# Hybrid attention and mLSTM block on one core: weights' sums, the norm of the far blocks and a gate moved in the program order

## The chip, the cores and the metric

The kernel runs on one core of a Trainium2 chip. The metric is the device time of one execution in microseconds (us), the median of the runs; lower is better. A core has a matrix engine (TensorE, PE in the profile, with its weight loads shown apart as PEld), a vector engine (VectorE, DVE), a scalar engine (ScalarE, ACT), GpSimd (POOL) and SyncE (SP), from which this kernel issues all its DMAs. Each engine works through its instructions in program order and waits on semaphores for the others.

## The reference, cut to what matters

```python
xn = rms_norm(x, mix_norm_g)                    # x: (1, 2048, 1024), one layer
aq, ak, av, mq, mk, mv, mo, i, f, ga, gm = split(xn @ w_in)
att = chunk_band_attention(aq, ak, av, rel_bias)          # 8 heads of 64, chunks of 64
hm = mlstm_chunkwise(silu(conv(mq)), silu(conv(mk)), mv, i + b_i, f + b_f)
hm = rms_norm(hm, mh_norm_g)                              # per head, 4 heads of 128
mlstm_out = sigmoid(mo) * hm
y = sigmoid(ga) * (att @ w_att_proj) + sigmoid(gm) * (mlstm_out @ w_mlstm_proj)
x = x + y @ w_out
x = x + square(relu(rms_norm(x) @ w_up)) @ w_down
out = rms_norm(x, final_norm_g)
```

Everything is float32. A matrix product is made of three products of float32r parts (high by high, high by low, low by high), so each operand is first split into two parts.

## The kernel before, in words

**Blocks and spans.** The 2048 tokens are four blocks of 512; two blocks are a span. Blocks 0 and 1 are projected plainly, one after the other (`dense`, L625): value tiles, gates, query, key and conv tiles, then `ga` tiles, then the two projections of the mixers. From there on both blocks of a span go together through products by a 2x2 scheme with seven products instead of eight (`quad`, L542): each quad is 7 products of 24 matmuls of 128x512, 168 in all. In order of time these stages are here called G0 and G1 (gate `gm` of the first span), O0 and O1 (`w_out` of the first span), then the second span's input projections gm0, gm1, q, mq, vm0, ga0, k, vm1, mk, ga1, mo (`IN_ORDER`, L51), then up0.0 to up0.7, the down products of the first span (`down`, L598) with the attention and the recurrence of blocks 2 and 3 beside them, and O1, up and down of the second span.

**Operands.** A quad needs seven combinations of the four quarters of its activations. `take_parts` (L1697) makes them: for each k of four it takes five tiles of the pool `ctx`, loads four quarters (L1706), scales them where a norm's gain is due (L1709), makes four sums on DVE (L1719) and splits each of seven into a tile pair (ACT L953, DVE L958). k above 1 waits until k - 2 is split. `norm_far` (L863) makes the normed input of blocks 2 and 3 for it: it loads 32 tiles of 256 KB, squares 16 of them on ACT, scales 16 on DVE (L899) and stores these 16.

**Weights.** They need the same seven combinations. There are two ways. The sum: `sum_w` (L374) loads the four quarters of half a quad (256 KB each, L384), makes four differences on DVE (L389) and stores them in DRAM (`wsum`); the loader then loads each of the seven parts (512 KB, L402). The second difference of a half waits until the first is stored. The quad form: `quad_w` (L426) loads the four quarters (512 KB, L397) into the four buffers `wraw` and makes the differences there on DVE (L439, 128x1024); for the up products of the first span it stores them too (`keep`, L434), since the second span loads them again. Either way each part is split by ACT (L420) and DVE (L422).

**Taking results off.** The banks of a quad are reused: `combine` (L1732) copies or adds a product into `ctx` (ACT L1742, DVE L1750), and the next product of that bank waits for it. `after_out` adds at L1987, `add_down` at L2187. For `mo`, `finish` of `after_in` (L1900) applies tanh on ACT (L1914) and then (t + 1) times a gain on GpSimd (L1919), and stores the tile to `mfar` (L2026).

**The order.** All of this is written as threads, and a planner (`Flow`, L92) decides in which order their instructions are written down: it keeps an estimated clock for each engine and takes the ready step that could start first; equal starts go by the thread's priority. Each step names its engine, an estimated duration and, for a load, an estimated time until it lands: `yield "sp", 900, 2000` is 0.9 us of issue and 2.0 us more to landing. A further layer then places the instructions on the engines. The estimates change no wait: they set the order alone. Side work (sums, `norm_far`) is spawned with a low priority at a point of `dense`: in the kernel before, `norm_far` after the mixer inputs of block 0 (L656), the sums of G and O weights at the end of block 0, those of the two `vm` quads at the end of block 1 (L666), and those of the eight down quads at the places `D_SUMS` (L53) of the second span's projections (L691) and of up0 (L711).

Of the kernel before, what the change touches and what calls it, by code (L numbers as in the profile page):

```python
# [51 lines left out]
N_REC = 1  # L52
D_SUMS = (3, 6, 9, 11, 12, 13, 14, 15)  # L53
PROJ = {2: (4,0), 3: (6,2)}
# [37 lines left out]
class Flow:  # L92
# [77 lines left out]
    def run(self):  # L170
        while self.ready or self.blocked:
            moved = True
            while moved:
                moved = False
                for th in sorted(self.blocked, key=lambda x: (x.prio, x.n)):
                    ok, value = self._grant(th)
                    if ok:
                        self.blocked.remove(th)
                        self.now = th.at
                        self._step(th, value)  # L180
                        moved = True
            if not self.ready and not self.blocked:
                break
            if not self.ready:
                raise RuntimeError("no thread can go on")
            best = None
            for th in self.ready:
                t, frm = th.at
                for e in th.req[0].split("|"):
                    start = t + self.LAT[frm].get(e, 0.0)  # L190
                    if e == "pe" and th.prio < 5:
                        start += self.SLACK
                    key = (max(self.clock[e], start), th.prio, th.n)
                    if best is None or key < best[0]:
                        best = (key, th, e)
            (start, _, _), th, e = best
            self.ready.remove(th)
            end = start + th.req[1]
            self.clock[e] = end
            if len(th.req) > 2:  # L200
                end += th.req[2]
            th.at = self.now = (end, e)
            self._step(th, e)


def act_ns(n, ps=False, ap=0):
    return (51 if ps else 93) + 0.834 * n + 93 * ap
# [11 lines left out]
class Layer:  # L219
# [98 lines left out]
    def weights(self):  # L318
# [13 lines left out]
        for s in range(NS):  # L332
            if s == 1:
                yield from (part(q, m) for q in range(N_G, N_G + N_O) for m in range(7))
            for q in range(N_G + N_O, N_G + N_O + N_F):
                if s == 0:
                    yield "quad", (q, True)
                else:
                    yield from (part(q, m) for m in range(7))
# [34 lines left out]
    def sum_w(self, q):  # L374

        fl, V = self.fl, self.nc.vector
        for h in range(2):
# [4 lines left out]
            for n, x in ((0, a), (1, c), (3, d), (2, b)):  # L382
                yield "sp", 900, 2000
                self.nc.sync.dma_start(x, wf[n])  # L384
# [240 lines left out]
    def dense(self):  # L625
        fl = self.fl
        none = [None] * KT
        for b in range(2):
# [25 lines left out]
            if b == 0:  # L654
                fl.spawn(self.norm_in(1), 3)
                fl.spawn(self.norm_far(), 3)  # L656
            for j in range(8):
# [4 lines left out]
            if b == 1:  # L662
                G = self.operands()
                for k in range(4):
                    fl.spawn(self.take_xn(0, k, *G), 2)
            early = range(N_G + N_O) if b == 0 else range(Q_VM, Q_VM + 2)  # L666
            for q in early:
                fl.spawn(self.sum_w(q), 3)
# [21 lines left out]
        for i, name in enumerate(IN_ORDER):  # L690
            if i in D_SUMS:  # L691
                fl.spawn(self.sum_w(N_Q - N_F + D_SUMS.index(i)), 3)
            last = name == IN_ORDER[-1]
# [9 lines left out]
        for s in range(NS):  # L703
# [6 lines left out]
            for i in range(N_F):  # L710
                if s == 0 and len(IN_ORDER) + i in D_SUMS:  # L711
                    fl.spawn(self.sum_w(N_Q - N_F + D_SUMS.index(len(IN_ORDER) + i)), 3)
                if i == 2:
# [983 lines left out]
    def take_parts(self, src, kept, scale, k, A, aev, g=None):  # L1697
        fl, V = self.fl, self.nc.vector
        if k > 1:
            yield "wait", [aev[m][k - 2] for m in range(7)]  # L1700
        got = yield "get", self.ctx, 5
        a11, a12, a21, a22, s1 = (x[:, :512] for x in got)
        for b, j, a in ((0, k, a11), (0, 4 + k, a12), (1, k, a21), (1, 4 + k, a22)):
            yield "wait", [kept[b][j]]
            yield "sp", 900, 2000
            self.nc.sync.dma_start(a, src[b].ap()[j])  # L1706
# [15 lines left out]
        yield "wait", done  # L1722
        fl.put(self.ctx, *got)

# [6 lines left out]
    def combine(self, finish, o=0):  # L1731
# [6 lines left out]
        def copied(n, name, ps, clear):  # L1738
            (t,) = yield "get", self.ctx, 1
            held[n][name] = t  # L1740
            yield "act", act_ns(512, True)
            nc.scalar.copy(t[:, o:o + 512], ps)  # L1742
# [3 lines left out]
        def summed(n, name, to, ps, clear):  # L1746
            yield "wait", [ev[n][name]]
            t = held[n][name]
            yield "dve", dve_ns(512)
            nc.vector.tensor_add(t[:, o:o + 512], ps, t[:, o:o + 512])  # L1750
# [148 lines left out]
    def after_in(self, name):  # L1899
        fl, nc = self.fl, self.nc  # L1900

        def finish(n, which, t, ps):
# [14 lines left out]
            if name == "mo":  # L1917
                yield "pool", 670
                nc.gpsimd.tensor_scalar(t5, t5, 1.0, self.ghead[:, j:j + 1], op0=ALU.add, op1=ALU.mult)  # L1919
                dst, ev = self.mfar[b].ap()[2 * MH + j], self.m_ev[b, 2 * MH + j]  # L1920
# [35 lines left out]
    def after_out(self, s, q, U):  # L1956
# [24 lines left out]
        def add(n, w, done, ps, clear):  # L1981
# [3 lines left out]
            t = xt[n][w][:, :512]  # L1985
            yield "dve", dve_ns(512)
            V.tensor_add(t, ps, t)  # L1987
# [177 lines left out]
    def add_down(self, s, m, j, ps):  # L2165
# [9 lines left out]
        else:  # L2175
# [7 lines left out]
            for to, frm in steps:  # L2183
                if to not in acc:
                    (acc[to],) = yield "get", self.ctx, 1
                yield "dve", dve_ns(512)
                V.tensor_add(acc[to][:, :512], ps, acc[frm][:, :512])  # L2187
# [128 lines left out]
    def build(self):  # L2316
# [19 lines left out]
        self.wev, self.wgot = collections.defaultdict(Event), collections.defaultdict(Event)  # L2336
        self.td_ev = {q: E(2) for q in (*range(N_G + N_O), *range(N_Q - N_F, N_Q + 2))}
        self.t_ev = [[E(4) for _ in range(7)] for _ in range(NS)]
# [112 lines left out]
```

## Time and profile before

| | |
|---|---|
| median of 3 runs | 2897.58 us (2896.61 to 2900.97) |
| the profiled execution | 2903.79 us |
| its span, first to last instruction | 2901.7 us |
| mean granted clock of TensorE | 0.993 |
| DMAs | 629.87 MB, queue q1 busy 65.4% of 16 engines' span |
| instructions of `sum_w`'s differences (L389) | 112, of quad form's (L439) 60 |

The page gives busy times by engine, groups of instructions by line, and for each the idle time of the engine before them with what ended it. The windows view gives the busy time, number of instructions and granted clock in any stretch; the waits view who waited for whom; the timeline single instructions with, in brackets, the idle time of their engine just before and what ended it.

### The profile page before, as it was taken

To read this page: it belongs to the slowest core of one execution; us is meant where nothing else is said; L and a number is where in the kernel's file an instruction comes from. 1 tells how busy PE (TensorE), PEld (TensorE's weight loads), DVE (VectorE), ACT (ScalarE), POOL (GpSimd) and SP (SyncE) were. 2 spreads that over 40 slices of the span, in tenths; PEclk is the share of its full clock that TensorE was granted. 3 is DMA by queue.
4 is the path that set the end of the run, shared out by engine and by line. 5 is a ranking of instruction groups with operands and counts; after the bars stand their busy time and mean duration, and the time that the engine had idled before them with its cause. 6 is when DMAs were issued, how large, how long until landed. Compare 5 with 4: busy or idle time off the path is not lost.

```text
span 2901.7 us, 39144 instructions
## 1 busy us (share of the span) xinstructions
PE 2827.3 (97%) x13576; PEld 2351.1 (81%) x13576; DVE 2035.9 (70%) x3778; ACT 1549.2 (53%) x2690; POOL 67.6 (2%) x124
## 2 busy tenths in 40 slices
PE   8999999999999999999999999999899999999998
PEld 7888878887787888877888888788778888888887
DVE  6886579867884865876666787769877744455565
ACT  4665356644453544565555575446645755554444
POOL 0000000000000000020000000000000000000000
PEclk9999999999999999999999999999999999999999
DMA  6328963368974566668877966688468855576563
GB/s 214 99 94 296 318 204 95 103 229 301 306 240 139 200 217 218 203 218 293 291 273 257 272 205 189 200 243 273 147 212 293 270 193 186 188 255 201 192 220 136
DMA packets 287238, 629.87 MB, mean 217 GB/s; under 512 B 31936, under 2 KB 46400, under 8 KB 287040
## 3 DMA queue, kind: packets, MB, share of 16 engines
q1 hardware_dynamic: 287040, 627.38, 65.4%
q8 instruction: 106, 1.74, 0.2%
q14 instruction: 92, 0.75, 0.1%
HBM read 437.46 MB, written 189.79 MB: 216 GB/s over the span
## 4 chain that ended last, share of the span: by engine, by line
PE 75%; DVE 10%; DMA 7%; ACT 4%; issue 3%; POOL 1%; SPq 0%; POOLq 0%; DVEq 0%; ACTq 0%
PE bank L564 33%; PE bank L481 11%; PE bank L482 11%; PE bank L483 11%; PE bank L592 2%; DVE wsp L422 2%; PE bank L1210 2%; PE bank L1245 1%; PE bank L1276 1%; DVE r L958 1%; DMA r<-u 1%; ACT wsp L420 1%; DMA wsum<-ctx 1%; DVE sc L1251 1%; DMA tmp<-in_x 1%
## 5 line engine op out<-in xcount | busy, mean ns | idle before, releaser
L564 PE MATMUL bank<-r,wsp 128*128 128x512 f32 x5208 | 1197.6, 391 | 22.0 <-DVE ctx L1750 9.6
L564 PEld LDWEIGHTS bank<-r,wsp 128*128 128x128 f32 x5208 | 979.7, 189 | 234.2 <-DVE ctx L1750 11.9
L422 DVE TENSOR_TENSOR wsp<-wraw,wsp 128x1024 fp32r<-128x1024 f32 x461 | 563.2, 1222 | 359.5 <-ACT wsp L420 349.2
L420 ACT CAST wsp<-wraw 128x1024 fp32r<-128x1024 f32 x461 | 484.0, 1050 | 526.7 <-PE bank L482 220.7
L481 PE MATMUL bank<-r,wsp 128*128 128x512 f32 x1600 | 640.0, 400 | 1.5 <-DVE scs L1251 0.8
L482 PE MATMUL bank<-r,wsp 128*128 128x512 f32 x1600 | 625.6, 391 | 0.0
L483 PE MATMUL bank<-r,wsp 128*128 128x512 f32 x1600 | 625.5, 391 | 0.0
L483 PEld LDWEIGHTS bank<-r,wsp 128*128 128x128 f32 x1600 | 300.7, 188 | 64.9
L481 PEld LDWEIGHTS bank<-r,wsp 128*128 128x128 f32 x1600 | 301.5, 188 | 54.3 <-DVE tmp L1222 1.2
L482 PEld LDWEIGHTS bank<-r,wsp 128*128 128x128 f32 x1600 | 301.8, 189 | 52.4 <-DVE r L958 0.2
L1750 DVE TENSOR_TENSOR ctx<-bank,ctx 128x512 f32<-128x512 f32 x174 | 118.6, 686 | 91.9 <-PE bank L564 90.3
L953 ACT CAST r<-r 128x512 fp32r<-128x512 f32 x224 | 136.6, 622 | 76.0 <-DMA r<-u 63.1
L958 DVE TENSOR_TENSOR r<-r 128x512 fp32r<-128x512 f32 x224 | 149.3, 687 | 36.5 <-ACT r L953 35.5
L1742 ACT COPY ctx<-bank 128x512 f32<-128x512 f32 x174 | 101.1, 582 | 68.1 <-PE bank L564 63.9
L1260 ACT ACTIVATE sc<-sc,scs 128x640 f32<-128x640 f32 (+4 forms) x128 | 97.4, 761 | 69.8 <-DVE scs L1257 68.5
L389 DVE TENSOR_TENSOR ctx<-ctx,ctx 128x512 f32<-128x512 f32 x112 | 76.4, 689 | 66.5 <-DMA ctx<-in_wf 37.9
L1210 PE MATMUL bank<-r,r 128*128 128x256 f32 (+1 forms) x672 | 111.1, 284 | 6.8 <-DVE r L1281 6.2
L2121 ACT ACTIVATE ctx<-ctx 128x512 f32<-128x512 f32 x96 | 60.6, 631 | 102.6 <-DVE ctx L1750 102.5
L1210 PEld LDWEIGHTS bank<-r,r 128*128 128x128 f32 x672 | 98.7, 191 | 20.2 <-DVE r L1281 9.9
L1251 DVE CUSTOM_DVE_ANT_0 sc<-bank,bias 128x320 f32<-128x320 f32 (+3 forms) x240 | 105.6, 459 | 7.8 <-PE bank L1245 6.8
L1281 DVE TENSOR_TENSOR r<-bank,r 128x512 fp32r<-128x512 f32 (+1 forms) x168 | 96.3, 593 | 10.4 <-ACT r L1279 9.7
L953 ACT CAST r<-ctx 128x512 fp32r<-128x512 f32 x116 | 69.5, 618 | 61.2 <-DMA ctx<-xn 30.2
(274 smaller groups left out, 2906.1 us busy)
## 6 DMA issues: line engine op xcount, KB each, us to landing
wraw<-in_wf SPq DMA_DIRECT2D x168, 512.0 KB, 4.2
wraw<-wsum SPq DMA_DIRECT2D x144, 512.0 KB, 4.1
r<-u SPq DMA_DIRECT2D x224, 256.0 KB, 4.2
wraw<-in_w SPq DMA_DIRECT2D x104, 512.0 KB, 3.8
u<-ctx SPq DMA_DIRECT2D x128, 256.0 KB, 2.7
ctx<-in_wf SPq DMA_DIRECT2D x112, 256.0 KB, 4.5
wsum<-ctx SPq DMA_DIRECT2D x112, 256.0 KB, 3.7
u<-tmp SPq DMA_DIRECT2D x96, 256.0 KB, 3.2
```

What stands on the lines that cost most here:

```text
L420: nc.scalar.copy(w[:, 0], raw)
L422: nc.vector.tensor_sub(w[:, 1], raw, w[:, 0].bitcast(F32))
L481: mm(ps, lh, rh, start=first, stop=False)
L482: mm(ps, lh, rl, start=False, stop=False)
L483: mm(ps, ll, rh, start=False, stop=last)
L564: mm(ps, wv[:, x, k, n], a[:, y], start=new and k == 0 and x == y == 0, stop=k == 3 and x == 1, skip_group_check=True)
L953: self.nc.scalar.copy(dst[:, 0], src)
L958: self.nc.vector.tensor_sub(dst[:, 1], src, dst[:, 0].bitcast(F32))
L1210: nc.tensor.matmul(bk[:, c0:c0 + w], st, sl[:, x, o:o + w], start=n == 0, stop=n == total - 1)
L1251: nc.vector.tensor_tensor_reduce(out=e[:, x * w:x * w + w], in0=bks[x][:, :w], in1=br[:, j0 + x * w:j0 + x * w + w], op0=ALU.add, op1=ALU. ...
L1742: nc.scalar.copy(t[:, o:o + 512], ps)
L1750: nc.vector.tensor_add(t[:, o:o + 512], ps, t[:, o:o + 512])
```

## The change

1. `norm_far` is spawned after the mixer inputs of block 1 and not of block 0.
2. The sums of the two `vm` quads are spawned at places 1 and 2 of the second span's projections, and not at the end of block 1.
3. The first two up quads of the first span (`N_USUM`) change from the quad form to sums, spawned at places 4 and 5; their parts are loaded seven by seven. The eight down sums move to places 7, 9 and 11 to 16.
4. The estimate of the landing of loads in `take_parts` and `sum_w` goes from 2000 to 3500 ns.
5. `take_parts` takes the five tiles of odd k from the pool `temp` (6 tiles) where the scale is 1.
6. Steps that free a bank (`combine`, `after_out`, `add_down`) go ahead of others that could start at the same time (`"dve!"`, `"act!"`: priority -1).
7. The gain of `mo` is applied on ACT (Identity with scale and bias g, that is g t + g) and not on GpSimd.

```diff
+N_USUM = 2
+EARLY_SUMS = {1: Q_VM, 2: Q_VM + 1, 4: N_G + N_O, 5: N_G + N_O + 1}
+EARLY_SUMS.update({i: N_Q - N_F + n for n, i in enumerate((7, 9, 11, 12, 13, 14, 15, 16))})
...
+                    prio = th.prio
+                    if e[-1] == "!":
+                        e, prio = e[:-1], -1
...
-                    key = (max(self.clock[e], start), th.prio, th.n)
+                    key = (max(self.clock[e], start), prio, th.n)
...
-                if s == 0:
+                if s == 0 and q >= N_G + N_O + N_USUM:
                     yield "quad", (q, True)
...
-                yield "sp", 900, 2000
+                yield "sp", 900, 3500
                 self.nc.sync.dma_start(x, wf[n])
...
             if b == 0:
                 fl.spawn(self.norm_in(1), 3)
+            else:
                 fl.spawn(self.norm_far(), 3)
...
-            early = range(N_G + N_O) if b == 0 else range(Q_VM, Q_VM + 2)
-            for q in early:
+            for q in range(N_G + N_O if b == 0 else 0):
                 fl.spawn(self.sum_w(q), 3)
...
-            if i in D_SUMS:
-                fl.spawn(self.sum_w(N_Q - N_F + D_SUMS.index(i)), 3)
+            if i in EARLY_SUMS:
+                fl.spawn(self.sum_w(EARLY_SUMS[i]), 3)
...
-        got = yield "get", self.ctx, 5
+        pool = (self.ctx, self.temp)[k % 2 if scale == 1.0 else 0]
+        got = yield "get", pool, 5
...
-            yield "sp", 900, 2000
+            yield "sp", 900, 3500
             self.nc.sync.dma_start(a, src[b].ap()[j])
...
-            yield "dve", dve_ns(512)
+            yield "dve!", dve_ns(512)
             nc.vector.tensor_add(t[:, o:o + 512], ps, t[:, o:o + 512])
...
             if name == "mo":
-                yield "pool", 670
-                nc.gpsimd.tensor_scalar(t5, t5, 1.0, self.ghead[:, j:j + 1], op0=ALU.add, op1=ALU.mult)
+                yield "act", act_ns(512, False, 2)
+                g = self.ghead[:, j:j + 1]
+                nc.scalar.activation(t5, t5, AF.Identity, scale=g, bias=g)
```

More of the change, by code (lines that the diff above doesn't have):

```diff
@@ L52 @@
 N_REC = 1
-D_SUMS = (3, 6, 9, 11, 12, 13, 14, 15)
+N_USUM = 2
+EARLY_SUMS = {1: Q_VM, 2: Q_VM + 1, 4: N_G + N_O, 5: N_G + N_O + 1}
+EARLY_SUMS.update({i: N_Q - N_F + n for n, i in enumerate((7, 9, 11, 12, 13, 14, 15, 16))})
 PROJ = {2: (4,0), 3: (6,2)}
@@ L710, in dense @@
             for i in range(N_F):
-                if s == 0 and len(IN_ORDER) + i in D_SUMS:
-                    fl.spawn(self.sum_w(N_Q - N_F + D_SUMS.index(len(IN_ORDER) + i)), 3)
+                if s == 0 and len(IN_ORDER) + i in EARLY_SUMS:
+                    fl.spawn(self.sum_w(EARLY_SUMS[len(IN_ORDER) + i]), 3)
                 if i == 2:
@@ L1722, in take_parts @@
         yield "wait", done
-        fl.put(self.ctx, *got)
+        fl.put(pool, *got)
     def take_split(self, src, m, k, A, aev, scale=1.0):
@@ L1740, in copied @@
             held[n][name] = t
-            yield "act", act_ns(512, True)
+            yield "act!", act_ns(512, True)
             nc.scalar.copy(t[:, o:o + 512], ps)
@@ L1985, in add @@
             t = xt[n][w][:, :512]
-            yield "dve", dve_ns(512)
+            yield "dve!", dve_ns(512)
             V.tensor_add(t, ps, t)
@@ L2185, in add_down @@
                     (acc[to],) = yield "get", self.ctx, 1
-                yield "dve", dve_ns(512)
+                yield "dve!", dve_ns(512)
                 V.tensor_add(acc[to][:, :512], ps, acc[frm][:, :512])
@@ L2336, in build @@
         self.wev, self.wgot = collections.defaultdict(Event), collections.defaultdict(Event)
-        self.td_ev = {q: E(2) for q in (*range(N_G + N_O), *range(N_Q - N_F, N_Q + 2))}
+        self.td_ev = {q: E(2) for q in (*range(N_G + N_O + N_USUM), *range(N_Q - N_F, N_Q + 2))}
         self.t_ev = [[E(4) for _ in range(7)] for _ in range(NS)]
```

## The prediction

> **What bounds the kernel now.** I read the page's busy times first.
>
> ```profile
> PE 2827.3 (97%) x13576; PEld 2351.1 (81%) x13576; DVE 2035.9 (70%) x3778; ACT 1549.2 (53%) x2690; POOL 67.6 (2%) x124
> ```
>
> TensorE is busy for 2827.3 of 2901.7 us, and the change leaves every matmul in place: the same seven products of the same weights, made another way. So all that can be won lies in the 74 us in which TensorE stands still and in the time in which its clock is low. The windows view says where; its columns are the stretch, its length, then busy time and number of instructions of PE, PEld, DVE, ACT, POOL, the granted clock and the DMA share.
>
> ```profile
> 250.00:300.00 50.00, 50.00 (x236) 41.76 (x235) 36.45 (x52) 17.32 (x24) 3.19 (x1) 1.00 0.94 314
> 350.00:420.00 70.00, 66.13 (x311) 54.68 (x310) 47.50 (x126) 31.64 (x58) 2.96 (x6) 0.95 0.73 241
> 661.00:707.00 46.00, 41.63 (x171) 32.16 (x171) 33.34 (x49) 22.66 (x36) 0.00 (x0) 0.96 0.83 291
> 745.00:793.00 48.00, 41.75 (x170) 32.55 (x169) 42.80 (x63) 20.11 (x30) 0.00 (x0) 0.93 0.93 311
> 881.00:1227.00 346.00, 345.24 (x1524) 284.84 (x1523) 236.08 (x319) 164.12 (x229) 0.00 (x0) 1.00 0.60 199
> 1227.00:1273.00 46.00, 39.73 (x168) 32.39 (x167) 37.27 (x50) 33.40 (x55) 15.69 (x7) 0.93 0.52 176
> 1273.00:1316.00 43.00, 39.94 (x169) 32.57 (x168) 32.16 (x41) 21.61 (x32) 1.75 (x1) 0.96 0.80 282
> 1316.00:1354.00 38.00, 38.00 (x168) 31.28 (x168) 26.59 (x33) 19.98 (x29) 0.00 (x0) 1.00 0.90 317
> 1588.00:2031.00 443.00, 435.92 (x2357) 372.08 (x2356) 348.29 (x848) 246.87 (x499) 9.87 (x36) 1.00 0.76 231
> 2031.00:2184.00 153.00, 138.42 (x745) 116.09 (x745) 124.92 (x278) 86.57 (x190) 4.86 (x8) 0.99 0.56 179
> ```
>
> A clean quad is 168 matmuls in 38.0 us (1316:1354), 0.226 us each. By that rate G0 (661:707) loses 46 - 171 x 0.226 = 7.3 us, O0 (745:793) 9.5, mo (1227:1273) 8.0, up0.0 (1273:1316) 4.8: 29.6 us in four quads. In 350:420, with the attention of block 1, PE is idle for 3.9 us, and a clock of 0.95 costs about 3.5 more: 7.4. Beside the far attention (1588 to 2184) it idles for 7.1 and 14.6 us. The stretch from gm1 to ga1 (881:1227) loses 0.8 us in 346, with DVE at 236: there is room.
>
> The waits view, TensorE's own waits in the windows around G0, O0, mo with up0.0, and 340:420 (what waited, for whom, us, times, longest):
>
> ```profile
> PE bank L564 <- ACT r L953: 2.8, 2, 2.0
> PE bank L564 <- DVE r L960: 3.5, 2, 3.3
> PE bank L564 <- ACT r L955: 2.3, 3, 0.9
> PE bank L564 <- DVE ctx L1750: 9.3, 2, 6.3
> PE bank L1245 <- DVE scs L1251: 3.9, 2, 2.7
> ```
>
> G0 and O0 wait for split operands (L953 to L960), mo and up0.0 for the additions that free a bank (L1750).
>
> **The change part by part.** *G0.* The timeline shows what its splits wait for:
>
> ```profile
> 663.92 0.62 ACT L953 CAST r<-ctx 128x512 fp32r<-128x512 f32 x1 [6.78 <-DMA ctx<-xn]
> 673.22 1.28 ACT L953 CAST r<-ctx 128x512 fp32r<-128x512 f32 x2 [6.76 <-DMA ctx<-xn]
> ```
>
> ACT stands twice for 6.8 us for loads of `take_parts`, while sums load and store beside them. Edit 2 takes the sums away (15 of their subtractions stood in the projections of block 1 and G0, with 11 loads and their stores on SP's queue), and edit 5 lets k = 2 and 3 load early: in the changed program's order all 16 loads and 16 additions stand ahead of G0, where 8 additions and 6 loads stood in it. G0 keeps 30 vector instructions of 48. What comes in is `norm_far`: 6 loads or stores and 6 squares. I take 5.5 of 7.3 us; bounds 0 (the wait only moves) and 7.3.
>
> *O0.* DVE is busy for 42.8 of 48 us, DMA for 0.93. The changed order has 50 vector instructions in O0 for 59, and 2 loads of the next operands for 8; against it stand 6 scalings of `norm_far` with 7 DMAs. The chain from G1's last product through tanh, two gate operations, sums and split stays. I take 4.5 of 9.5; bounds 0 and 9.5. If the cover is gone it shows one stage on: in O1 and gm0 the operands of block 2 and 3 follow `norm_far` more closely (11 of 16 additions in O1, 8 before).
>
> *mo.* The timeline, in order of time:
>
> ```profile
> 1242.08 6.21 POOL L1919 TENSOR_SCALAR ctx<-ctx,ghead 128x512 f32<-128x512 f32 x1 [0.80 <-ACT ctx L1914]
> 1248.32 0.32 SPq L2026 DMA_DIRECT2D mfar<-ctx  x1
> 1248.73 1.97 SPq L1706 DMA_DIRECT2D ctx<-x  x3
> 1251.33 0.72 ACT L1709 ACTIVATE ctx<-ctx,gcol 128x512 f32<-128x512 f32 x1 [3.29 <-DMA ctx<-x]
> 1265.97 9.26 PE L564 MATMUL bank<-r,wsp 128*128 128x512 f32 x32 [6.27 <-DVE ctx L1750]
> ```
>
> One GpSimd multiply takes 6.21 us; the store of its tile holds SP's queue until 1248.3; the loads of the up operands stand behind it, ACT (L1709) waits for them, DVE's sums for ACT, and the bank-freeing L1750 behind those. Edit 7 removes that:
>
> ```profile
> L1919 POOL TENSOR_SCALAR ctx<-ctx,ghead x8: 692/1732/6209, 1239.2 to 1274.9; 128x512 f32<-128x512 f32 x8
> L1941 ACT ACTIVATE ctx<-ctx,cvw x16: 802/817/821, 968.5 to 1190.3; 128x512 f32<-128x512 f32 x16
> ```
>
> Eight multiplies of 0.7 to 6.2 us become eight ACT instructions. The nearest row, the conv's Identity with scale and bias by column, gives 0.82 us: 6.5 us more on ACT, which is busy for 33.4 of 46 us there, ahead of the copies that free banks. I take 6 of 8.0; bounds -2 (a third of the new ACT time in TensorE's way) and 8.0.
>
> *up0.0, and edits 3, 4 and 6.* Its stall is a sum's:
>
> ```profile
> 1304.05 1.42 DVE L389 TENSOR_TENSOR ctx<-ctx,ctx 128x512 f32<-128x512 f32 x2 [5.43 <-DMA wsum<-ctx]
> 1309.11 16.18 PE L564 MATMUL bank<-r,wsp 128*128 128x512 f32 x63 [3.06 <-DVE ctx L1750]
> ```
>
> DVE waits 5.43 us for the store of a half's first difference, and L1750 stands behind it. Edit 4 touches the landing of loads, not of this store. But the first two up quads leave the quad form:
>
> ```profile
> L389 DVE TENSOR_TENSOR ctx<-ctx,ctx x112: 678/691/695, 252.9 to 1489.6; 128x512 f32<-128x512 f32 x112
>   DMA ctx<-in_wf: 37.9, 23
>   DMA wsum<-ctx: 25.6, 15
> L439 DVE TENSOR_TENSOR wraw<-wraw,wraw x60: 1210/1218/1633, 912.3 to 1556.9; 128x1024 f32<-128x1024 f32 x60
> ctx<-in_wf SPq DMA_DIRECT2D x112, 256.0 KB, 4.5
> wsum<-ctx SPq DMA_DIRECT2D x112, 256.0 KB, 3.7
> ```
>
> They lose 8 x 1.22 = 9.8 us of DVE and 8 stores of 512 KB at this place, and gain 16 x 0.69 = 11.0 us with 16 loads and 16 stores of 256 KB in earlier quads, and 14 part loads for 8 (30 DMAs more on SP in all). I take 2 of 4.8; bounds -4 (a second such stall) and 4.8.
>
> *Sums in gm0 to ga1.* By program order 48 subtractions stand there, 24 before. 24 more make 16.5 us of DVE, 236 to about 253 of 346 us. At the idle time of L389's own rows, (37.9 + 25.6)/112 = 0.57 us each, another 14 go in waiting. The slack of 110 us covers that on the average; but gm0 comes to 62 vector instructions for 52. I take 5 us of loss; bounds 0 and 15.
>
> *350:420.* DMA is at 0.94 in 250:300, where `norm_far` runs beside the sums. The changed order has 15 of its DMAs late in block 1, and none here. I take 3 of 7.4; bounds -4 and 7.4, since the attention units stand in another order.
>
> *Far attention.* No edit aims at it, but the planner's clocks shift and its order with them. Before, 232 attention and recurrence matmuls stand in one piece without a dense one, late in the down products, where 14.6 us are idle; after, 109 and 86 in two pieces. The idle time goes with such pieces: 14.6 x 195/232 = 12.3. I take 2; bounds -10 and 10.
>
> *Sum.* 5.5 + 4.5 + 6 + 2 + 3 + 2 - 5 = 18. The profiled execution took 2903.8 us, 2.1 over its span and 6.2 over the median of the runs. The difference is taken over: 2897.6 - 18 = **2879.6 us**.
>
> [...]
>
> **The rivals.** *The estimate does nothing.* In the changed program's order 41 of 128 subtractions still stand within 3.5 us of TensorE's work behind their load (35 of 112 before), some at 2.5, where loads take 4.5. So edit 4 hardly reaches the engines, and the operands' waits could come back at O1 and gm0. Then only mo is won: 6 for mo, minus 5 for sums, and 3 of the rest: 2897.6 - 4 = 2893.6. For it speaks that order; against it that the loads of G0 do stand earlier.
>
> *The far attention pays.* The piece of 109 at the first far projection is new. If it costs as much as the old one, 14.6 more instead of 2 won: 2879.6 + 16.6 = 2896.2. Against it: vector work is spread more evenly there.
>
> *Slower: a sum at the head of DVE's queue.* A subtraction waiting for a load or its half's first store blocks the L1750 behind it; the case at 1304 cost 4.8 us. The 48 in gm0 to ga1 are 12 halves. The other terms give 23 us, so with five such stalls nothing is left, and from six on, 6 x 4.8 = 29, it is slower: 2897.6 - 23 + 29 = 2903.6. At nine it is 2918. For it: short distances in gm0, q and ga0, and gm0's load. Against it: 24 of them cost TensorE 0.8 us at most in 881:1227.
>
> **How the numbers follow.** Forecast 0.64, the idle estimate 0.10, the far attention 0.06, a sum ahead of bank-freeing 0.20. A measurement of this kernel can tell about 0.2% (5.8 us) from no change: below 2891.8 is faster, above 2903.4 slower. So faster 0.64, same 0.16, slower 0.20. With all upper bounds but the far attention's the gain is 7.3 + 9.5 + 8.0 + 4.8 + 7.4 + 2 = 39, which gives 2858.6, and the slower case from six to seven stalls 2903.6 to 2908; I give **2858 to 2908**, which leaves out some 0.04 below and 0.15 above. The forecast's own range is 2858 to 2891.
>
> **What would show it.** G0 and O0 near 38 us with at most 2 us of idle time; no POOL row for `ghead` in mo and no wait of L1709 for loads behind an `mfar` store; up0.0 without L439; 881:1227 still without PE idle time, though L389 waits more in all; two shorter idle pieces by the far projections. A stall over 3 us in gm0 or q with L1750 behind L389 would make it wrong, as would a later end of the far attention.

## The result, and the profile after

The changed kernel takes **2881.31 us** (median of 4 runs, 2878.25 to 2887.80); the kernel before took 2898.64 us on the same chip (4 runs, 2896.61 to 2900.97). The ratio is **0.9943, with a 95% interval of 0.9924 to 0.9962**. The forecast was 2879.6 us. The profiled execution of the changed kernel took 2887.8 us, its span 2886.0, so its stages carry some 6 us more than the median. The profile of before lies 5.2 us above its own.

The first row of the page, the busy times:

```profile
PE 2825.3 (98%) x13576; PEld 2352.4 (82%) x13576; DVE 2036.1 (71%) x3785; ACT 1559.5 (54%) x2699; POOL 46.5 (2%) x116
```

The matmuls are the same in number. POOL lost 21 us and eight instructions (mo's gain), ACT gained 10 us.

The windows view of the changed kernel, each row laid over the same quad or stretch as in the prediction, from its first matmul to that of the next one (columns as there). In this order: the stretch with block 1's attention, G0, O0 with a part of O1, gm1 to ga1, vm1 alone, mo, up0.0, and the far attention in two parts:

```profile
345.00:415.00 70.00, 68.55 (x343) 57.05 (x343) 49.27 (x137) 34.08 (x62) 2.04 (x3) 1.00 0.48 169
649.40:695.40 46.00, 41.23 (x170) 33.51 (x170) 25.19 (x33) 21.35 (x40) 0.00 (x0) 0.93 0.86 285
734.90:782.90 48.00, 43.80 (x188) 34.38 (x187) 41.27 (x60) 17.80 (x24) 0.00 (x0) 1.00 0.91 313
866.80:1215.70 348.90, 346.44 (x1522) 285.57 (x1521) 249.84 (x340) 170.22 (x238) 0.00 (x0) 1.00 0.64 223
1097.50:1139.50 42.00, 39.96 (x169) 32.59 (x169) 27.28 (x32) 21.26 (x28) 0.00 (x0) 0.96 0.89 304
1215.70:1255.00 39.30, 38.68 (x169) 31.37 (x168) 35.07 (x49) 32.96 (x52) 0.00 (x0) 1.00 0.78 266
1255.00:1297.40 42.40, 39.86 (x169) 32.57 (x168) 28.61 (x41) 25.82 (x40) 0.00 (x0) 0.96 0.80 266
1570.70:2013.00 442.30, 432.39 (x2354) 369.86 (x2353) 352.10 (x875) 252.84 (x524) 10.33 (x37) 0.98 0.72 225
2013.00:2166.30 153.30, 145.60 (x744) 121.31 (x743) 122.00 (x250) 81.48 (x165) 4.25 (x6) 0.98 0.58 194
```

The first matmul of G0 now comes at 649.4 us instead of 661.0, and mo fits into 39.3 us. But G0 still takes 46 us, vm1 42, up0.0 42.4: there TensorE stands still again, and three of these rows have a clock of 0.93 to 0.96. TensorE's waits in the whole span (what waited, for whom, us, times, longest):

```profile
PE bank L570 <- DVE ctx L1757: 10.8, 7, 4.8
PE bank L570 <- ACT r L961: 4.1, 2, 2.7
PE bank L598 <- DVE ctx L1757: 2.5, 2, 2.0
```

L1757 is the addition that frees a bank (L1750 before). Its 9.3 us in mo and up0.0 have become 10.8 on L570 and 2.5 on L598, at other places. The timeline has three of them. In G0:

```profile
674.30 0.63 ACT L882 ACTIVATE tmp<-tmp 128x512 f32<-128x512 f32 x1 [4.04 <-DMA tmp<-in_x]
...
676.90 1.03 ACT L426 CAST wsp<-wraw 128x1024 fp32r<-128x1024 f32 x1
...
677.96 1.23 DVE L428 TENSOR_TENSOR wsp<-wraw,wsp 128x1024 fp32r<-128x1024 f32 x1 [6.57 <-ACT wsp L426]
679.10 0.69 DVE L1757 TENSOR_TENSOR ctx<-bank,ctx 128x512 f32<-128x512 f32 x1
679.12 0.63 ACT L882 ACTIVATE tmp<-tmp 128x512 f32<-128x512 f32 x1 [0.71 <-DMA tmp<-in_x]
...
679.87 1.67 SPq L1849 DMA_DIRECT2D tmp<-proj  x2
...
685.67 0.69 DVE L1853 TENSOR_TENSOR ctx<-ctx,tmp 128x512 f32<-128x512 f32 x1 [1.43 <-DMA tmp<-proj]
686.28 0.69 DVE L1757 TENSOR_TENSOR ctx<-bank,ctx 128x512 f32<-128x512 f32 x1
...
687.02 13.25 PE L570 MATMUL bank<-r,wsp 128*128 128x512 f32 x45 [4.77 <-DVE ctx L1757]
```

L882 is the squaring of `norm_far`. ACT stands at it for 4.04 us, because its input has not landed. The cast of the next weights (L426) is queued behind it, DVE's L428 waits 6.57 us for that cast, and L1757 stands behind L428. Six us later DVE waits once more: L1853, an addition of the gate, stands for a load of `proj`, with the next L1757 behind it, and TensorE is out of banks for 4.77 us. That load is issued only at 679.87 and lands 5.7 us later. Ahead of it SP's queue stood 1.4 us for a buffer that the late L428 frees, and then 0.2 us for a tile that the square held: squares and loads of `proj` take their tiles from the same pool, `temp`, and between 664 and 690 SP waits for squares 2.6 us in four such waits. So the norm reaches G0 in more ways than by ACT's queue, and which costs most, no run separates. In vm1:

```profile
1125.16 0.73 ACT L1716 ACTIVATE tmp<-tmp,gcol 128x512 f32<-128x512 f32 x1 [1.88 <-DMA tmp<-x]
...
1128.72 0.72 ACT L1716 ACTIVATE tmp<-tmp,gcol 128x512 f32<-128x512 f32 x1 [1.89 <-DMA tmp<-x]
1129.35 2.08 ACT L426 CAST wsp<-wraw 128x1024 fp32r<-128x1024 f32 x2
1130.41 1.23 DVE L428 TENSOR_TENSOR wsp<-wraw,wsp 128x1024 fp32r<-128x1024 f32 x1 [1.00 <-ACT wsp L426]
1131.55 1.28 DVE L1757 TENSOR_TENSOR ctx<-bank,ctx 128x512 f32<-128x512 f32 x2
...
1132.38 3.88 PE L598 MATMUL bank<-wsp,r 128*128 128x512 f32 x10 [2.04 <-DVE ctx L1757]
```

It is the first of these chains again: ACT waits for a load, the cast is late, DVE waits, a bank comes late. This time the load is an operand of the up quads, which now may go to the pool `temp` (edit 5). Only the third one, in up0.0, is a sum at the head of DVE's queue (L395 is the difference of `sum_w`, L389 before):

```profile
1285.23 1.42 DVE L395 TENSOR_TENSOR ctx<-ctx,ctx 128x512 f32<-128x512 f32 x2 [4.50 <-DMA ctx<-in_wf]
...
1286.57 0.68 DVE L1757 TENSOR_TENSOR ctx<-bank,ctx 128x512 f32<-128x512 f32 x1
...
1288.30 1.41 DVE L395 TENSOR_TENSOR ctx<-ctx,ctx 128x512 f32<-128x512 f32 x2
...
1289.63 1.28 DVE L1757 TENSOR_TENSOR ctx<-bank,ctx 128x512 f32<-128x512 f32 x2
...
1290.37 2.07 PE L570 MATMUL bank<-r,wsp 128*128 128x512 f32 x4 [2.54 <-DVE ctx L1757]
```

### The profile page after: what moved, and what is told of

The parts are those of the page before. It is cut to its first block, busy times and chain, and to the rows that moved or that the text cites. A ratio compares the mean times of both kernels' runs of the same rounds, so it can differ in the third digit from the quotient of the medians.

```text
span 2886.0 us, 39211 instructions
## 1 busy us (share of the span) xinstructions
PE 2825.3 (98%) x13576; PEld 2352.4 (82%) x13576; DVE 2036.1 (71%) x3785; ACT 1559.5 (54%) x2699; POOL 46.5 (2%) x116
## 4 chain that ended last, share of the span: by engine, by line
PE 77%; DVE 9%; DMA 8%; ACT 3%; issue 2%; SPq 0%; POOL 0%; POOLq 0%; DVEq 0%; ACTq 0%
PE bank L570 32%; PE bank L487 12%; PE bank L488 12%; PE bank L489 11%; PE bank L598 2%; PE bank L1216 2%; DVE wsp L428 2%; PE bank L1251 2%; PE bank L1282 2%; DMA ctx<-in_wf 1%; DMA r<-u 1%; DVE r L964 1%; DMA wsum<-ctx 1%; ACT wsp L426 1%; DMA proj<-tmp 1%
## 5 line engine op out<-in xcount | busy, mean ns | idle before, releaser
L570 PE MATMUL bank<-r,wsp 128*128 128x512 f32 x5208 | 1194.9, 391 | 17.3 <-DVE ctx L1757 10.8
L570 PEld LDWEIGHTS bank<-r,wsp 128*128 128x128 f32 x5208 | 978.1, 188 | 227.8 <-DVE ctx L1757 14.1
L428 DVE TENSOR_TENSOR wsp<-wraw,wsp 128x1024 fp32r<-128x1024 f32 x461 | 564.0, 1223 | 348.6 <-ACT wsp L426 327.0
L426 ACT CAST wsp<-wraw 128x1024 fp32r<-128x1024 f32 x461 | 484.2, 1050 | 496.7 <-PE bank L570 193.3
L1757 DVE TENSOR_TENSOR ctx<-bank,ctx 128x512 f32<-128x512 f32 x174 | 119.2, 688 | 90.3 <-PE bank L570 90.3
L959 ACT CAST r<-r 128x512 fp32r<-128x512 f32 x224 | 136.5, 622 | 67.5 <-DMA r<-u 57.9
L395 DVE TENSOR_TENSOR ctx<-ctx,ctx 128x512 f32<-128x512 f32 x128 | 87.4, 690 | 68.8 <-DMA ctx<-in_wf 48.0
L1282 PE MATMUL bank<-const,sc 128*128 128x128 f32 x560 | 84.7, 280 | 12.2 <-DVE tmp L1228 5.3
```

The source lines that it names most:

```text
L426: nc.scalar.copy(w[:, 0], raw)
L428: nc.vector.tensor_sub(w[:, 1], raw, w[:, 0].bitcast(F32))
L570: mm(ps, wv[:, x, k, n], a[:, y], start=new and k == 0 and x == y == 0, stop=k == 3 and x == 1, skip_group_check=True)
L959: self.nc.scalar.copy(dst[:, 0], src)
L1282: nc.tensor.transpose(bk[:, o:o + P], prob[i][0][:, c:c + P], self.ident)
```

## The experiments

The theory after the result: two parts of the change make the gain, the place of the sums of vm's weights (edit 2) and mo's gain on ACT (edit 7). The norm's new place (edit 1) only moves a loss from the blocks into G0, and the rest cancels out. The rivals: edits 4 to 6 carry a good part; the added sums make the new stalls; the estimate does nothing.

Each ratio is taken to runs of the kernel before on the same chip, so kernels are compared by ratios; a median belongs to its own chip. The stages come from the one profiled execution of each kernel. "To G0" is G0's first matmul; "G0-O1", "gm0-ga1", "up" (up0.0 to up0.7) and "far" (the down products of the first span, with the far attention) are lengths in us.

| kernel | median us | ratio, 95% | to G0 | G0 | G0-O1 | gm0-ga1 | mo | up | far |
|---|---|---|---|---|---|---|---|---|---|
| before | 2898.6 | | 661.0 | 45.8 | 172.0 | 393.9 | 46.3 | 315.1 | 595.7 |
| changed | 2881.3 | 0.9943 (0.9924-0.9962) | 649.4 | 46.0 | 167.5 | 398.8 | 39.3 | 315.7 | 595.6 |
| e1 edit 7 alone | 2890.8 | 0.9961 (0.9946-0.9975) | 658.0 | 44.1 | 169.6 | 394.1 | 41.1 | 309.6 | 596.8 |
| e2 edit 1 undone | 2876.7 | 0.9916 (0.9902-0.9930) | 658.6 | 38.1 | 155.7 | 399.8 | 38.6 | 313.4 | 592.5 |
| e3 edit 2 undone | 2898.6 | 0.9988 (0.9977-0.9998) | 648.2 | 52.8 | 184.0 | 401.4 | 40.4 | 313.2 | 589.0 |
| e4 edit 4 undone | 2884.5 | 0.9936 (0.9923-0.9949) | 647.1 | 46.4 | 171.9 | 398.4 | 39.2 | 316.2 | 590.9 |
| e5 edits 2, 7 alone | 2884.7 | 0.9936 (0.9922-0.9950) | 656.3 | 38.1 | 156.5 | 399.5 | 40.1 | 309.3 | 601.6 |
| e6 edit 6 undone | 2882.4 | 0.9937 (0.9923-0.9951) | 648.1 | 46.3 | 170.3 | 395.9 | 39.0 | 319.6 | 587.9 |
| e7 edit 3 undone | 2880.2 | 0.9928 (0.9914-0.9942) | 648.0 | 45.5 | 168.6 | 397.4 | 38.7 | 311.5 | 589.9 |
| e8 edit 5 undone | 2886.1 | 0.9949 (0.9934-0.9965) | 649.2 | 44.5 | 170.7 | 396.1 | 38.5 | 316.7 | 589.3 |
| e9 half of 5 undone | 2881.4 | 0.9929 (0.9914-0.9944) | 649.3 | 42.2 | 169.5 | 395.1 | 38.5 | 317.3 | 589.9 |
| e10 edits 1, 3, half of 5 undone | 2877.2 | 0.9918 (0.9904-0.9932) | 659.9 | 38.1 | 155.6 | 395.9 | 38.4 | 313.3 | 591.0 |
| e11 as e10, norm split | 2870.0 | 0.9893 (0.9877-0.9908) | 654.4 | 38.1 | 157.2 | 395.2 | 39.1 | 313.4 | 588.2 |
| e12 edits 1, 3, 5 undone | 2878.1 | 0.9917 (0.9903-0.9930) | 655.0 | 38.1 | 156.2 | 395.2 | 42.0 | 312.8 | 594.3 |

Three comparisons show how far such lengths scatter. e1 has the order of before up to mo, and yet reaches G0 3.0 us earlier. e7 and e9 have the order of the changed kernel up to q and vm1, and yet their G0 takes 45.5 and 42.2 us for 46.0, and G0 to O1 168.6 and 169.5 for 167.5. And "far" is 588.2 to 595.6 us in nine kernels (the changed one, e2, e3, e7 to e12) whose first down product takes 57.9 us in each, while it takes 62 to 66 in the others.

**e1.** The kernel before, with edit 7 alone:

```
-                yield "pool", 670
-                nc.gpsimd.tensor_scalar(t5, t5, 1.0, self.ghead[:, j:j + 1], op0=ALU.add, op1=ALU.mult)
+                yield "act", act_ns(512, False, 2)
+                g = self.ghead[:, j:j + 1]
+                nc.scalar.activation(t5, t5, AF.Identity, scale=g, bias=g)
```

> The kernel before with one part of the change: mo's gain by an ACT Identity with scale and bias by column instead of GpSimd's multiply; nothing else. My theory (GpSimd's 6.21 us multiply held the store, the loads behind it and so the bank-freeing addition): mo falls from 46.4 us to 39 to 41, with under 1 us of idle time, up to mo the stages keep their lengths within 0.5 us, up0.0 stays near 43 or loses a part of its 4.8 us, and the whole is 5 to 9 us shorter, ratio 0.9969 to 0.9983. Rival (it was the change's other parts, the sums and the priority of bank-freeing steps, that cleared mo): mo stays above 44 us, the whole within 3 us of before.

Measured 2890.75 us, 10.3 below before, where the theory had 5 to 9. The windows of mo and up0.0:

```profile
1221.70:1262.80 41.10, 38.40 (x170) 31.47 (x169) 35.83 (x49) 36.06 (x59) 0.00 (x0) 1.00 0.60 194
1262.80:1300.80 38.00, 38.00 (x169) 31.49 (x168) 31.40 (x42) 24.03 (x37) 0.00 (x0) 1.00 0.90 322
```

mo falls by 5.2 us, with 2.7 of idle time left (more than the 1 us expected). What the expectation left open is the larger surprise: **up0.0 becomes a clean quad**, 38.0 us instead of 43.1, with its weights in the old form and DMA at 0.90. Its stall went with mo's. From mo on the planner's order differs from before's, so whether up0.0 was cured by the time or by the order of its sums is not separated. From gm0 to the down products, e1 takes 744.8 us, before 755.3: edit 7 is worth some 10 us, and the ratio says 11 (7 to 16).

**e2.** The norm spawned after block 0's inputs again:

```
             if b == 0:
                 fl.spawn(self.norm_in(1), 3)
-            else:
                 fl.spawn(self.norm_far(), 3)
```

> The changed kernel with the norm of blocks 2 and 3 spawned after block 0's mixer inputs again, as before. If the norm's new place gave the 11.6 us that the two blocks won (it ran beside the sums in block 0 and 1), the blocks take 661 us up to G0 again, and G0 loses its new idle piece of 4.8 us and O0 its 4.2, so that the total is 2 to 4 us above the changed kernel. If taking the sums of vm's weights out of block 1 gave it, the blocks stay at 649 to 652 us, G0 and O0 come to 38 to 40 us, and the total is 6 to 11 us below the changed kernel.

Both halves came, one from each theory: the blocks take 658.6 us again, and G0 is clean. G0 and O0:

```profile
658.60:696.70 38.10, 38.10 (x169) 31.53 (x168) 23.21 (x30) 17.56 (x26) 0.00 (x0) 1.00 0.82 271
735.20:775.40 40.20, 38.56 (x170) 31.40 (x169) 35.98 (x53) 15.78 (x24) 0.00 (x0) 1.00 0.96 324
```

So the norm in block 1 wins 9.2 us up to G0 and loses 11.8 in G0 to O1. By the ratios e2 is some 8 us faster than the changed kernel; the intervals overlap, so that edit 1 on its own is not shown to cost time, but no gain of it is left either. Two later pairs with the norm in block 1 and in block 0 (e9 and e10, e8 and e12; edit 3 differs too) say the same: it wins 10.6 and 5.8 us up to G0 and loses 13.9 and 14.5 in G0 to O1.

**e3.** The sums of vm's weights at the end of block 1 again:

```
-EARLY_SUMS = {1: Q_VM, 2: Q_VM + 1, 4: N_G + N_O, 5: N_G + N_O + 1}
+EARLY_SUMS = {4: N_G + N_O, 5: N_G + N_O + 1}
...
-            for q in range(N_G + N_O if b == 0 else 0):
+            for q in range(N_G + N_O) if b == 0 else range(Q_VM, Q_VM + 2):
```

> The changed kernel with the sums of vm's two weight quads spawned at the end of block 1 again, as before; the norm of blocks 2 and 3 stays in block 1. Theory 1 (the norm gave the blocks' 11.6 us): the blocks stay at 649 to 652 us, gm0, gm1 and q lose what the sums cost them (1 to 2 us), G0 gets 3 sums beside the norm and takes 46 to 50 us, total within 5 us of the changed kernel. Theory 2 (the absence of these sums gave it): block 1 takes 6 to 9 us more, the total is 5 to 12 us above the changed kernel.

2898.57 us: of the gain 0.12% is left. The total is worse than either theory had it, and the place is a third one: the blocks stay at 648.2, but G0 takes 52.8 us and G0 to O1 184.0. The timeline of G0:

```profile
683.46 0.63 ACT L882 ACTIVATE tmp<-tmp 128x512 f32<-128x512 f32 x1 [9.21 <-DMA tmp<-in_x]
684.09 1.03 ACT L426 CAST wsp<-wraw 128x1024 fp32r<-128x1024 f32 x1
685.15 1.23 DVE L428 TENSOR_TENSOR wsp<-wraw,wsp 128x1024 fp32r<-128x1024 f32 x1 [4.92 <-ACT wsp L426]
685.65 3.02 PE L570 MATMUL bank<-r,wsp 128*128 128x512 f32 x12 [2.81 <-ACT ctx L1749]
```

The chain of the changed kernel's G0 is here with a wait of 9.21 us at its head. The load of this square is issued only at 679.48: SP's queue stood 3.9 us at a store of the norm, which waited for its own scaling on DVE. With the sums beside the norm G0 takes 52.8 us, with the norm alone 46.0 (changed), with the sums alone 45.8 (before), with neither 38.1 (e2). By which queue the sums add to it is not shown.

**e4.** `yield "sp", 900, 2000` for 3500 in `sum_w` and `take_parts`.

> The changed kernel with the landing estimate of the loads of operands and weights' differences at 2000 instead of 3500 ns. The traces show 4.5 us for these loads. If the estimate matters as meant, the subtractions and additions stand nearer behind their loads, L395 waits for its loads more than the 48.0 us of the changed kernel (60 or more), and TensorE gets new waits behind L1757: total 5 to 15 us above the changed kernel. If it hardly reaches the program's order, L395's idle time stays within 10 us of it and the total within 4 us, either way.

What L395 waits for, in the answer for that line (us, times), in the changed kernel and here:

```profile
  DMA ctx<-in_wf: 48.0, 26
```

```profile
  DMA ctx<-in_wf: 73.5, 33
```

The estimate reaches the program: DVE's sums wait 25 us longer without it. But the ratio is 0.9936, not to be told from the changed kernel's. The first theory is right in its first half alone: TensorE's waits for L1757 are 11.9 us in 6 against 10.8 in 7, so the longer waits hardly pass on to it. The prediction's rows had shown room on DVE from gm1 to ga1.

**e5.** The kernel before with edit 7 as in e1 and edit 2 alone:

```
-            early = range(N_G + N_O) if b == 0 else range(Q_VM, Q_VM + 2)
-            for q in early:
+            for q in range(N_G + N_O if b == 0 else 0):
...
+            if i in (1, 2):
+                fl.spawn(self.sum_w(Q_VM + i - 1), 3)
```

> The kernel before with two parts of the change alone: the sums of vm's two weight quads taken from the end of block 1 to the first places of the second span's projections, and mo's gain on ACT. The norm of blocks 2 and 3, the landing estimate, the pool of the operands, the priority of bank-freeing steps and the up quads' form stay as before. Theory 1 (these two parts make the gain, the rest adds nothing on balance): G0 starts at 657 to 660 us and takes 38 to 40, gm0 starts at 813 to 820 (833.0 before, 816.9 changed), mo takes 39 to 42, and the total is 2874 to 2886 us, not above the changed kernel by more than 3. Theory 2 (the other parts carry half of it: operands loaded early, priority): gm0 starts at 822 us or later, the total is 2887 to 2893.

2884.68 us, 0.9936: **two edits give the whole gain**. G0 takes 38.1 us, gm0 starts at 812.8, up0.0 takes 38.2. Against the changed kernel's profile it loses 6.9 us up to G0 and 6.0 in the far attention, whose order is another one, and gains 11.0 in G0 to O1 and 6.4 in the up quads.

**e6.** `"act!"` and `"dve!"` without the mark.

> The changed kernel without the priority of the bank-freeing steps, all else as changed. If the priority pays, TensorE waits more for L1757 and L1995 than in the changed kernel (10.8 us in 7 waits and 0.4 in one), in O0, mo and up0.0 above all, and the total is 3 to 8 us above it. If the planner's order would have put those steps there anyway, these waits stay within 3 us of that and the total within 4 us, either way, with the far attention's stretch differing by as much as its own order does.

```profile
PE bank L570 <- DVE ctx L1757: 15.1, 8, 4.8
```

TensorE waits 4.3 us more for L1757, in up0.2 to up0.4, which take 40.3, 41.5 and 42.3 us. That the priority works there is seen in this one profile; that it pays is not: the ratio is 0.9937, and gm0 to ga1 and the far attention are shorter by 2.9 and 7.7.

**e7.** `N_USUM = 0`, and no places 4 and 5 in `EARLY_SUMS`.

> The changed kernel with all up quads of the first span in the quad form again, so 16 subtractions fewer in q to ga0. My theory (moving them costs little in q to ga0 and relieves up0.0): q to ga1 stay within 1 us of the changed kernel's, vm1's new idle piece of 2.0 us among them or gone, up0.0 and up0.1 lose 1 to 4 us more, total 0 to 4 us above the changed kernel. Rival (the added sums are what made the new stalls of vm1 and up0.0): vm1 takes 38.7 instead of 42.0 and up0.0 38 to 40 instead of 42.4, total 3 to 7 us below the changed kernel.

The two up quads, here and in the changed kernel:

```profile
1252.70:1330.20 77.50, 76.44 (x337) 62.97 (x336) 59.98 (x77) 46.14 (x71) 0.00 (x0) 1.00 0.84 296
```

```profile
1255.00:1336.80 81.80, 78.29 (x338) 64.04 (x337) 53.36 (x72) 46.02 (x70) 0.00 (x0) 0.98 0.83 289
```

The new form has less work for DVE there (53.4 us for 60.0) and yet takes 4.3 us more: it doesn't relieve up0.0. How much it costs varies. up0.0 and up0.1 together take 77.7 to 82.0 us in the seven kernels with edit 3, and 76.3 to 78.3 in the six that have edit 7 without it (e1, e5, e7, e10 to e12). up0.0's whole stall needs more than edit 3: it takes 42.4 and 42.6 us in the changed kernel and e8, and 38.4 to 40.1 in the other five. vm1 improves only to 39.7. The total is not told apart from the changed kernel's.

**e8.** `pool = self.ctx` in `take_parts`, for every k.

> The changed kernel with the operands of every k from one pool again. If the second pool pays, as the prediction had it, O0 to gm0 or G0 wait for operands: G0 to gm0 take 5 us or more above the changed kernel's 217.4 us, by waits for splits (L959 to L964). If it took the tiles that the norm of blocks 2 and 3 needs, and so drew that norm out into G0 and O0, the norm's DMAs stand earlier (20 of 23 in block 1 by the planner's order instead of 16), G0's idle piece of 4.8 us is 1 to 4 us shorter, and G0 to gm0 take the same or up to 6 us less.

Between the two: G0 to gm0 takes 220.4 us against 217.4, vm1 38.7 against 42.0, 2886.1 us in all. The second pool loses 3.3 us in vm1. That it wins at G0 to gm0 is not shown: e9, which has the changed kernel's order there, takes 219.0 us.

**e9.** The second pool for the norms' operands alone:

```
-        pool = (self.ctx, self.temp)[k % 2 if scale == 1.0 else 0]
+        pool = (self.ctx, self.temp)[k % 2 if scale == 1.0 and g is None else 0]
```

> The changed kernel with one thing undone: the up operands (the loads that ACT scales, L1716) come from one pool again for every k; the operands from the norms keep both. The changed kernel's timeline shows ACT standing twice for 1.9 us in vm1 for these loads, its cast of the weights late for that, and the bank-freeing L1757 behind L428. Theory (that is the whole of vm1's new 2.0 us of idle time and the low clock after it): vm1 takes 38.7 us instead of 42.0, G0 to k as changed within 1 us, total 2 to 5 us below the changed kernel, unless mo and up0.0, where these loads now stand, give it back. Rival (the added sums are the cause): vm1 stays above 41 us.

vm1, then up0.3:

```profile
1099.00:1137.70 38.70, 38.30 (x169) 31.44 (x168) 25.71 (x31) 20.05 (x26) 0.00 (x0) 1.00 0.88 304
1370.10:1411.90 41.80, 40.01 (x169) 32.60 (x168) 26.89 (x34) 20.26 (x30) 0.00 (x0) 0.96 0.85 301
```

vm1 is clean, as the theory says: its stall came from the up operands loaded early. The other kernels agree. Where ACT scales such operands in vm1 (changed, e2, e3, e6, e7), TensorE stands still there for 1.3 to 2.2 us; where it doesn't (e4, e8, e9), vm1 takes 38.7. Without the added sums (e7) 1.4 us of the 2.0 stay. Some 3.7 us are given back in up0.3, where the order is another one: the total is not told apart from the changed kernel's.

**e10.** e2, e7 and e9 together.

> The changed kernel with three things undone: the norm of blocks 2 and 3 after block 0's mixer inputs, the up operands from one pool, all up quads of the first span in quad form. If the three are independent, as the stages so far say: gm0 starts at 813 to 816 us, vm1 takes 38.7, up0.0 to up0.2 114 to 118 together, and the total is 2867 to 2876 us, below both the changed kernel and the run with only the norm moved back (2876.7). If the planner's order makes them trade with each other, the total is 2877 to 2885.

gm0 starts at 815.5, vm1 takes 38.7 and up0.0 to up0.2 115.3, all as if independent; but up0.3 loses 2 us, and the ratio is that of e2. The two profiled spans differ by 3.6 us in e10's favour, but e2's profiled execution lies 4.1 us above its median and e10's at it. So whether the repairs trade with one another is not settled.

**e11.** As e10, with one block's norm in each block:

```
             if b == 0:
                 fl.spawn(self.norm_in(1), 3)
-            else:
-                fl.spawn(self.norm_far(), 3)
+            fl.spawn(self.norm_far(2 + b), 3)
...
-    def norm_far(self):
+    def norm_far(self, b):
...
-        for b in (2, 3):
+        for b in (b,):
```

> As the run with three things undone, but the norm of block 2 spawned in block 0 and that of block 3 in block 1. In the planner's order 31 of its 32 DMAs then end ahead of G0, where the changed kernel has 16 of them in G0 to O0. If a norm beside the sums is what block 0 and 1 lose, by its density, halves cost less: G0 starts at 653 to 657 us (658.6 with the whole norm in block 0, 649.4 with it in block 1), G0 takes 38 to 40, the total is 2 to 5 us below the run with three things undone. If only the amount of side work in the blocks counts, G0 starts at 658 to 660 us, the total is within 2 us of that run.

G0 and O0 of e11, in the windows view:

```profile
654.40:692.50 38.10, 38.10 (x170) 31.55 (x169) 23.38 (x31) 17.55 (x26) 0.00 (x0) 1.00 0.81 281
732.50:773.10 40.60, 38.60 (x170) 31.41 (x170) 36.11 (x53) 16.09 (x24) 0.00 (x0) 1.00 0.94 325
```

**2869.98 us, a ratio of 0.9893 (0.9877 to 0.9908)**: below both kernels, and its interval ends ahead of where the changed kernel's begins. On the same chip its five runs (2868.84 to 2873.47) all lie below e10's (2876.11 to 2881.93). G0 starts at 654.4, 5.5 us ahead of e10's, and is as clean; the far attention is 2.8 us shorter, which is within its scatter. That spreading the norm made the start earlier is likely but not shown: e12, with the whole norm in block 0, starts G0 at 655.0.

**e12.** As e10 with one pool for all operands.

> As the run with three things undone, but all operands from one pool, so that of the change there remain the sums' place, the landing estimate, the priority and mo on ACT. If the second pool pays for the operands of G0 and gm0 (the reason why it was forecast to help), O1 and gm0 take 2 us or more above that run's and the total is 2 to 5 us above it. If it does nothing there, G0 to gm0 and the total stay within 2 us of it.

G0 to O1 take 156.2 us against 155.6, so the second pool does nothing there once the norm is out of the way; block 1 (from 320 us to some 43 us before G0) is 4.4 us shorter without it (291.6 for 296.0), and mo 3.6 longer (42.0 for 38.4). The total is the same.

## Why the prediction was right, step by step

The total was right: 18 us forecast, 17.3 measured between the medians and 15.7 between the two profiled spans. Of its steps, some were right and two large ones wrong in opposite directions, so that the total came out so close is in part luck.

| step | forecast | between the two profiles | what the runs show |
|---|---|---|---|
| 350:420, blocks | 3 | 11.6 | mis-sized: edit 1, undone in e2 (9.2 of it) |
| G0 | 5.5 | -0.2 | wrong: edit 2 wins 7.7 (e5), edit 1 takes it back (e2) |
| O0 | 4.5 | 5.6 with O1 | right, for edit 2 (e5: 8.6) |
| mo | 6 | 7.0 | right: edit 7 (e1: 5.2) |
| up0.0 | 2 | 0.7 | wrong cause: edit 7 wins 5 (e1), most of it lost again, in part by edit 3 (e7) |
| sums in gm0 to ga1 | -5 | -4.9 | size right, cause only in part: 3.3 is vm1's operands (e9 loses 1.2 in all, e5 5.7) |
| far attention | 2 | 0.1 | nothing; scatter of some 6 us |

The rows add up to 19.9 us. What is missing to 15.7 was lost in stages that had no term: 0.9 in G1, 1.3 in up0.1 to up0.7 and 2.1 in the second span.

**The step that failed** is G0's: "What comes in is `norm_far`: 6 loads or stores and 6 squares. I take 5.5 of 7.3". The prediction named what comes in, and priced it at 1.8 us. It costs 7.9: 46.0 us against 38.1 in e2 (42.2 in e9, with the order of the changed kernel, so 4 to 8). A square is short (0.63 us), but it waits for a load at the head of ACT's queue (4.04 us for the one at 674.30), and the weights' cast stands behind it; SP's queue and the tiles of `temp` add to that (2.6 us in four waits for squares). The lower bound, "the wait only moves", is what happened. Edit 4 left the landing estimate of `norm_far`'s own loads at 2000 ns, while the load of the square at 674.30 was issued at 669.83 and took 4.5 us; what 3500 would do there is untested. All five kernels with neither this norm's squares nor vm's sums in G0 take 38.1 us there (e2, e5, e10 to e12); all seven with edit 1, the changed one among them, 42.2 to 52.8. The same edit's gain was mis-sized on the other side: 3 us for one window, where the two blocks together won 6 to 12. Before, L389 waited there for its loads at the head of DVE's queue, ahead of the scores (L1251) that TensorE then waited for:

```profile
389.80 0.69 DVE L389 TENSOR_TENSOR ctx<-ctx,ctx 128x512 f32<-128x512 f32 x1 [3.36 <-DMA ctx<-in_wf]
...
392.72 0.69 DVE L389 TENSOR_TENSOR ctx<-ctx,ctx 128x512 f32<-128x512 f32 x1 [1.50 <-DMA ctx<-in_wf]
...
399.05 0.80 PE L1245 MATMUL bank<-r,r 128*128 128x320 f32 x2 [2.71 <-DVE scs L1251]
```

With the norm gone from there, the DMA share of the stretch falls from 0.73 to 0.48, and TensorE's idle time in it from 3.9 to 1.5 us.

**mo** went as described: no multiply on POOL, and 0.6 us of idle time. **up0.0** was taken for a stall of its own sums. It went with mo's (e1), and the re-formed up quads, which the prediction credited with 2 us, win nothing there (e7). The two errors hid each other.

**The rivals.** "The estimate does nothing" is wrong in its mechanism (73.5 against 48.0 us of waits in e4); but no price of the estimate can be told from the noise either. The loads of the sums took 4.5 us from issue to landing (median of `ctx<-in_wf`), in the changed kernel as before. "The far attention pays" did not come. "A sum at the head of DVE's queue" came once in the changed kernel, in up0.0, with 2.54 us of idle time and not 4.8. The mechanism of the other new stalls was not on the list: **a load at the head of ACT's queue**, with 4.04 us of waiting in G0 and 1.88 and 1.89 in vm1, reaching TensorE by way of the cast, L428 and the bank, and in G0 also by SP's queue and the tiles of `temp`.

Open stays what each of edits 3 to 6 is worth alone: undone one by one they change the ratio by what would be 4 us less to 2 us more, within the intervals. That the far attention's order matters at all isn't settled either; its lengths differ as much between kernels with one order as between orders.

## What to carry to other kernels

Where engines work through their queues in order, price a piece of moved side work by the wait at its head and by what is queued behind it, not by its own duration. Here six squares of 0.63 us cost a quad 4 to 8 us, through three engines. Before a stall is put down to the work beside it, remove the stall ahead of it: with one edit in mo up0.0's went as well. When several edits come together, run those alone that the trace supports (e5), and divide the work that only moves its cost between the places (e11).

## What the runs showed of the hardware

The length of an idle gap did not tell whether the clock would drop. In e1 TensorE stood still for 1.40 us, and the granted clock was 0.79 over the 8 us around that gap; in e5 it stood still for 3.35 us, and the clock was 1.00 over the 14 us around it. The gap's row in the timeline and the stretch in the windows view, for e1:

```profile
398.29 1.19 PE L1245 MATMUL bank<-r,r 128*128 128x320 f32 x6 [1.40 <-DVE scs L1251]
```

```profile
396.00:404.00 8.00, 6.27 (x24) 5.03 (x25) 7.53 (x30) 3.13 (x7) 0.00 (x0) 0.79 0.63 203
```

For e5:

```profile
851.65 1.67 PE L564 MATMUL bank<-r,wsp 128*128 128x512 f32 x6 [3.35 <-DVE ctx L1751]
```

```profile
846.00:860.00 14.00, 10.65 (x47) 6.50 (x45) 8.23 (x11) 7.00 (x11) 0.00 (x0) 1.00 0.90 307
```

What made the difference, these rows don't show.

In vm1 and up0.0 of the changed kernel, with gaps of 2.04 and 2.54 us, the clock was 0.96 over 42.0 and 42.4 us. In e9 vm1 takes 38.7 us, with 0.4 us of idle time and a clock of 1.00. Of the 3.3 us between the two, 1.6 are idle time and 0.04 x 42 = 1.7 the clock, an estimate from the two rows. So the stall of 2.04 us cost vm1 more than its length, and e1's gap of 1.40 us shows that a shorter one did not always keep the clock up.
